# A feed-forward down projection in three parts, two of them by Strassen's seven products

## The chip, the core and the metric

The kernel runs on one core of a Trainium2 chip. A core has a matrix engine (PE) that multiplies a stationary 128x128 tile with moving columns and adds the result up in PSUM, a vector engine (DVE), an activation engine (ACT), a general engine (POOL), and a sync engine (SP) that here issues nearly all DMAs. Each has a queue of its own that runs in order; they wait for each other by semaphores. SBUF is the working memory. The metric is the time of one execution on the device in microseconds; lower is better.

## What is computed

One inference step of a one-layer decoder for 512 prompt tokens and 8 x 4 sample tokens, 544 in all, with d_model 1024 and d_ff 2816. Three token mixers run first; the change touches only the feed-forward part behind them:

```
u = _rmsnorm(x, ln_ffn) @ w_up              # (L, 1024) @ (1024, 5632)
u, ffn_conv_new = _causal_conv(u, ffn_conv, ffn_conv_w)
ua, ub = jnp.split(u + ffn_conv_b, 2, axis=-1)
x = x + ((jax.nn.silu(ua) * ub) @ w_down)   # (L, 2816) @ (2816, 1024)
return _rmsnorm(x, ln_final)
```

All data are float32.

## The kernel before

Tokens lie along the columns as two halves of 272 (256 prompt and 16 sample tokens each), features along the 128 partitions. `w_up` has 44 blocks of 128 output features with 8 k-tiles; `w_down` has 8 blocks with 22 k-tiles. The 22 feature tiles of the hidden layer are called features here: each needs two up products, one for `ua` and one for `ub`.

**A product with three matmuls.** Every float32 operand is split into a high part in the reduced type fp32r and the rest: ACT copies x to `hi`, DVE subtracts `lo = x - hi` (`split`, L252, and `wsplit`, L174, for weights). A product takes three matmuls per k-tile and half: hi·hi, hi·lo, lo·hi (`step`, L201). `gemm` (L187) does this over all k-tiles and both halves into a PSUM tile of two banks (`pm`, two such tiles); a second pool `p1` has four single banks (`bank`, L129).

**Weights.** `weights` (L159) loads up to 8 k-tiles with one DMA on SP into a `raw` tile (two buffers), and splits four k-tiles at a time into `whi` and `wlo` (four buffers each). The split of four k-tiles is one ACT and one DVE instruction of 512 columns. Loads and splits are placed ahead of their use by lowering the scheduler's priority number (`AHEAD` = 400).

**Order.** PE's instructions go in the order in which the program states them (`order`). The other queues are ordered by a list scheduler with a simulated timeline; `soon` gives what reads PSUM a priority 500 earlier. `gen` (L132) takes a scratch tile from a rotating pool `gp` of 30 in this part; `touch` (L135) writes one element of it with a POOL memset, so that POOL's queue holds the wait until that tile is free.

**The feed-forward loop** (`ffn`, L1461) has two parts of 11 features. For each feature: two up products, each with its side work (`ffn_side`, L1441: DVE scales out of PSUM into `U`, POOL copies the convolution's state in and out, ACT and two DVE instructions do the convolution), then silu on ACT, a product on DVE, and a split into `hi` and `lo`. Behind the 11 features come down products over these 11 k-tiles: all 8 blocks in the first part, blocks 0 to 5 in the second. Each result is added by DVE to the residual `xn[d]`. In the second part ACT squares the finished `xn[d]` and POOL sums the squares.

**The tail** (L1510 to L1534) does blocks 6 and 7 of the second part with the tokens in two groups of 312 and 232 columns: all matmuls of the first group, then those of the second, among which the first group's final normalisation (`final_norm`, L1543) is put at fixed points (`TK`, L1593: after k-tile 4 of block 6, and after k-tiles 1 and 2 of block 7). The second group's normalisation stands at the end by itself.

Of the kernel before, what the change touches and what calls it, by code (L numbers as in the profile page):

```python
# [9 lines left out]
F32 = mybir.dt.float32  # L10
# [12 lines left out]
NT = 4  # L23
HALF = 272
# [35 lines left out]
class Build:  # L60
# [140 lines left out]
    def step(self, o, w, r, hf, k, kt, first=True):  # L201

        (wh, wl), (rh, rl) = w, r
        self.mm(o, wh, rh[:, hf, :], start=(k == 0 and first), stop=False)
        self.mm(o, wh, rl[:, hf, :], start=False, stop=False)
        self.mm(o, wl, rh[:, hf, :], start=False, stop=(k == kt - 1))


# [1232 lines left out]
    def ffn_side(self, ps, i):  # L1441
# [17 lines left out]
        return y  # L1459

    def ffn(self):  # L1461
        self.lab = "_ff_"
        I = self.I
        KH = NPAIR // 2
        for part in range(2):
            acts = []
            for jj in range(KH):
                j = part * KH + jj
                pa = yield from self.gemm(I["wup"][j], self.h2)
                if j == 0:  # L1470
                    raw = self.gen((128, 2, HALF))
                    with self.soon():
                        self.act(raw, pa)
                    pa = raw
                    self.RB = self.rstd_rows(self.rs2, self.sqp.tile([128, 2, HALF], F32, tag="rbc", name="rbc"))
                ya = self.ffn_side(pa, j)
                pb = yield from self.gemm(I["wup"][NPAIR + j], self.h2)
                yb = self.ffn_side(pb, NPAIR + j)
                sg = self.yp.tile([128, 568], F32, tag="sg", name="sg")[:, 0:560]
                self.act(sg, ya, AF.Silu)  # L1480
                a = self.gen((128, 2, HALF))
                self.mul(a[:, :, 0:HP], self.two(sg[:, 0:512]), self.two(yb[:, 0:512]))
                vw = lambda t: t[:, 512:560].rearrange("p (a b t) -> p a b t", a=2, t=6)[:, :, :, 2:6]
                self.mul(a[:, :, HP:HALF].rearrange("p a (b t) -> p a b t", t=NT), vw(sg), vw(yb))
                hi, lo = self.gen((128, 2, HALF), F32R), self.gen((128, 2, HALF), F32R)
                self.split(a, hi, lo)
                acts.append((hi, lo))
            if part == 1:
                self.sy.dma_start(out=self.O["fc"], in_=self.fso)
                sqs = self.sqp.tile([128, 2, HALF], F32, tag="sqs", name="sqs")  # L1490
            for d in range(8 - 2 * part):
                ps = yield from self.gemm(I["wdn"][d][:, part * KH:(part + 1) * KH, :], acts)
                x = self.xn[d]
                with self.soon():
                    self.add(x, ps, x)
                if part == 0:
                    continue
                if d == 0:
# [13 lines left out]
        ds = (6, 7)  # L1512
        w = [self.weights(I["wdn"][d][:, KH:, :], KH, alt) for d in ds]
        ps = [self.pm.tile([128, 2, 512], F32, tag="mm", name="mm_fl_") for d in ds]
# [95 lines left out]
    def run(self):  # L1610
        with self.pool("cst") as self.cst, self.pool("wp") as self.wp, self.pool("hp", 8) as self.hp, \
# [15 lines left out]
            with self.pool("gp", self.NG1) as self.gp:  # L1627
# [179 lines left out]
```

## Time and profile before

| | |
|---|---|
| time, median of 3 runs | 1130.48 us (1130.06 to 1131.14) |
| profiled execution | 1130.19 us |
| its span | 1128.4 us |
| mean granted PE clock | 0.999 |
| HBM read and written | 98.93 and 11.21 MB |

The span is what the trace covers, from the first instruction to the last. A page line of busy time gives the engine, busy microseconds, the share of the span and the instructions. A row of instruction groups gives the line (often a helper's), engine, operation, output<-inputs, partitions x columns, count | busy us, mean ns of one | idle us before them and what ended the idle time. A row of windows gives the stretch, its length, and the busy us of PE, PE's weight load, DVE, ACT and POOL with their instruction counts, then the granted clock, DMA share and GB/s. A row of the chain or of the timeline gives start, length, engine, what, count. Matmuls are pipelined: one shows as about 0.29 us, but they start one behind the other at a smaller distance, so counts and stretches are used for them.

The feed-forward part runs from about 700 us on, with the stretches of up products and down products clearly apart in the slices of the page:

```profile
DVE  7886588777768657688653274476774337767533
ACT  6564344524426333353323244354443234444431
POOL 3000041100011103111321002122220012221112
PEclk9999999999999999999999999999999999999999
```

### The profile page before, as it was taken

How to read it: one execution, taken by the hardware profiler on the slowest of the kernel's cores; microseconds unless marked ns; L12 is line 12 of the kernel's file. 1: busy time of each engine (PE TensorE's matmuls, PEld its weight loads, DVE VectorE, ACT ScalarE, POOL GpSimd, SP SyncE). 2: the span in 40 equal slices, each digit the busy share in tenths (PEclk: the TensorE clock that was granted, in tenths of full speed). 3: DMA queues.
4: the chain of work that ended last, by engine and by line, in shares of the span. 5: the costliest groups of instructions: out<-in, count | busy, mean ns of one | idle time of the engine just before them, and what ended most of it. 6: DMA issues, size and time to landing. Idle time of an engine off the chain costs nothing.

```text
span 1128.4 us, 23470 instructions
## 1 busy us (share of the span) xinstructions
PE 1118.3 (99%) x9059; PEld 1101.7 (98%) x9059; DVE 732.1 (65%) x1827; ACT 466.5 (41%) x919; POOL 185.8 (16%) x664
## 2 busy tenths in 40 slices
PE   9999999999999999999999999999999999999997
PEld 8999999999999999999999999999999999999997
DVE  7886588777768657688653274476774337767533
ACT  6564344524426333353323244354443234444431
POOL 3000041100011103111321002122220012221112
PEclk9999999999999999999999999999999999999999
DMA  7233333232223334312453432323223333222332
GB/s 261 76 90 98 87 112 106 82 89 76 69 83 95 117 95 128 130 58 64 122 168 90 153 97 93 93 76 94 82 76 96 86 94 94 84 86 83 94 102 80
DMA packets 49831, 111.65 MB, mean 99 GB/s; under 512 B 11320, under 2 KB 17592, under 8 KB 49720
## 3 DMA queue, kind: packets, MB, share of 16 engines
q1 hardware_dynamic: 49000, 109.32, 31.7%
q8 instruction: 71, 1.16, 0.4%
q10 hardware_dynamic: 720, 0.84, 0.2%
q14 instruction: 40, 0.33, 0.1%
HBM read 98.93 MB, written 11.21 MB: 98 GB/s over the span
## 4 chain that ended last, share of the span: by engine, by line
PE 95%; DVE 2%; issue 1%; DMA 1%; ACT 1%; POOL 0%; SPq 0%; POOLq 0%; ACTq 0%; DVEq 0%
PE mm_fl__14143 L122 1%; PE mm_ff__11801 L122 1%; PE mm_ff__11633 L122 1%; PE mm_ff__11465 L122 1%; PE mm_ff__13687 L122 1%; PE mm_ff__14039 L122 1%; PE mm_ff__13863 L122 1%; PE mm_ff__13599 L122 1%; PE mm_ff__11297 L122 1%; PE mm_ff__13951 L122 1%; PE mm_ff__13775 L122 1%; PE mm_ff__11885 L122 1%; PE mm_ff__11717 L122 1%; PE mm_ff__11549 L122 1%; PE mm_ff__11381 L122 1%
## 5 line engine op out<-in xcount | busy, mean ns | idle before, releaser
L117 ACT ACTIVATE whi<-raw 128x512 fp32r<-128x512 f32 x320 | 199.5, 625 | 422.6 <-DMA raw<-in_wdn 11.7
L96 DVE TENSOR_TENSOR wlo<-raw,whi 128x512 fp32r<-128x512 f32 x320 | 221.1, 692 | 157.2 <-ACT whi L117 149.2
L114 DVE SCALAR_TENSOR_TENSOR y<-U,cols,y 128x560 f32<-128x560 f32 (+1 forms) x124 | 100.0, 808 | 19.0 <-ACT y L117 17.2
L117 ACT ACTIVATE y<-U,cols 128x560 f32<-128x560 f32 (+1 forms) x56 | 46.8, 838 | 23.6 <-DVE U L96 22.9
L1452 POOL COPY fso<-U 128x2 f32<-128x2 f32 x44 | 28.8, 654 | 79.6 <-DVE U L96 79.6
L1449 POOL COPY U<-fst 128x16 f32<-128x16 f32 x44 | 23.9, 546 | 81.4 <-DVE y L114 43.0
L117 ACT ACTIVATE sg<-y 128x560 f32<-128x560 f32 (+1 forms) x34 | 22.9, 675 | 21.0 <-DVE y L114 20.9
L114 DVE SCALAR_TENSOR_TENSOR col<-col,col 128x4 f32<-128x4 f32 (+3 forms) x146 | 24.7, 170 | 5.3 <-ACT junk L117 2.2
L117 ACT ACT_TABLE_LOAD x16 | 20.5, 1283 | 2.0 <-PEq L1799 0.7
L96 DVE TENSOR_TENSOR col<-col 128x4 f32<-128x4 f32 (+3 forms) x73 | 11.6, 158 | 1.3
L617 POOL COPY gso<-U 128x3 f32<-128x3 f32 x12 | 5.6, 464 | 23.0 <-ACT U L117 23.0
L111 DVE TENSOR_SCALAR col<-col 128x4 int32<-128x4 int32 (+4 forms) x32 | 6.8, 213 | 3.4 <-ACT junk L117 2.9
L96 POOL TENSOR_TENSOR tot<-tot 128x32 f32<-128x32 f32 (+5 forms) x25 | 7.8, 311 | 6.0 <-DVE gen_ph__5478 L96 3.8
L139 POOL MEMSET gen_ff__12393<- 1x1 f32 x1 | 0.1, 88 | 51.9 <-PE mm_ff__11885 L122 51.9
L1453 POOL COPY fso<-U 128x16 f32<-128x16 f32 x44 | 8.5, 193 | 0.0
L139 POOL MEMSET gen_bh__9001<- 1x1 f32 x1 | 0.1, 88 | 47.4 <-DVE gen_bh__8753 L96 47.4
L614 POOL COPY U<-gst 128x24 f32<-128x24 f32 x12 | 4.4, 373 | 20.7 <-DVE gen_g__2550 L96 8.9
L114 DVE SCALAR_TENSOR_TENSOR hlo<-xn,cols,hhi 128x544 fp32r<-128x544 f32 x8 | 6.3, 784 | 1.8 <-ACT hhi L117 1.8
L109 DVE TENSOR_SCALAR col<-col 128x4 int32<-128x4 int32 (+4 forms) x38 | 6.4, 169 | 0.7
L117 ACT ACTIVATE hhi<-xn,cols 128x544 fp32r<-128x544 f32 x8 | 6.0, 752 | 1.5 <-DVE xn L96 1.5
L122 PE MATMUL mm_fi__268<-rh 128*128 128x272 f32 x18 | 4.5, 441 | 1.3 <-DVE ones L1620 1.3
L114 DVE SCALAR_TENSOR_TENSOR xin<-xin,rp,gen_nr__470 128x544 f32<-128x544 f32 x8 | 5.7, 782 | 0.0
(5094 smaller groups left out, 4772.4 us busy)
## 6 DMA issues: line engine op xcount, KB each, us to landing
raw<-in_wp SPq DMA_DIRECT2D x47, 512.0 KB
raw<-in_wup SPq DMA_DIRECT2D x44, 512.0 KB
raw<-in_wgt SPq DMA_DIRECT2D x24, 512.0 KB
raw<-in_wdn SPq DMA_DIRECT2D x16, 512.0 KB
raw<-in_wbr SPq DMA_DIRECT2D x24, 256.0 KB
raw<-in_wout SPq DMA_DIRECT2D x8, 512.0 KB
raw<-in_wdn SPq DMA_DIRECT2D x16, 192.0 KB
xin<-in_xt SPq DMA_DIRECT2D x8, 272.0 KB
```

The source lines that it names most:

```text
L96: (eng or self.v).tensor_tensor(out=out, in0=a, in1=b, op=op)
L109: (eng or self.v).tensor_scalar(out=out, in0=a, scalar1=s1, scalar2=None, op0=op0)
L111: (eng or self.v).tensor_scalar(out=out, in0=a, scalar1=s1, scalar2=s2, op0=op0, op1=op1)
L114: self.v.scalar_tensor_tensor(out=out, in0=a, scalar=sc, in1=b, op0=op0, op1=op1)
L117: self.s.activation(out=out, in_=a, func=func, **kw)
L122: self.pe.matmul(out, lhsT=lhsT, rhs=rhs, start=start, stop=stop)
L139: self.g.memset(x[(slice(0, 1),) * len(x.shape)], 0.0)
L614: self.g.tensor_copy(out=sv[:, :, 0:3], in_=self.gst[:, tile_i, :, :])
L617: self.g.tensor_copy(out=self.gso[:, tile_i, 0, :], in_=U[:, 512:515])
L1449: self.g.tensor_copy(out=sv[:, :, 0:2], in_=self.fst[:, i, :, :])
L1452: self.g.tensor_copy(out=self.fso[:, i, 0, :], in_=U[:, 512:514])
L1453: self.g.tensor_copy(out=self.fso[:, i, 1:9, :], in_=sv[:, :, 4:6])
```

## The change

The 22 features are done in three parts of 8, 8 and 6. In the first two, the down product goes through Strassen's scheme with seven products in place of eight: two blocks of `w_down` by two k-tiles form a 2x2 matrix of 128x128 tiles, and two k-tiles by two token halves form the 2x2 matrix on the other side. For each pair of k-tiles (two features) `operands` builds seven right-hand sides: b11, b21, b22 of the activations themselves, four differences of which POOL does the subtractions, all split into `hi` and `lo`; they lie in tiles of a new pool `op` (eight tiles of 7 x 272 columns). For each pair of blocks `blocks` loads the 8 k-tiles of both blocks (one `raw` tile in `wp`, one in a new pool `wp2`, two buffers each) and forms four sums of weights, three on POOL and one on DVE. `seven` then runs the seven products, each 12 matmuls of 272 columns into one `p1` bank, with the weights' splits three products ahead. `adder` adds each product to the quarters of `xn` that need it: POOL does six additions per pair of blocks, DVE five with an operand in PSUM, ACT two copies out of PSUM.

The first feature of the next part (two up products and their side work) is moved ahead of a part's seven products. The third part's six features are split as before and its down products use `gemm` with six k-tiles; the tail has six k-tiles too. The scratch pool shrinks from 30 to 13.

```diff
+    SEVEN = ("a11", 0), ("s2", 4), ("s1", 3), ("s3", 5), ("a12", 1), ("s4", 2), ("a22", 6)
+
+    def operands(self, x0, x1, hi, lo):
+        t = self.gen((128, 2, HALF)), self.gen((128, 2, HALF))
+        b11, b12, b21, b22 = x0[:, 0, :], x0[:, 1, :], x1[:, 0, :], x1[:, 1, :]
+        self.sub(t[0][:, 0, :], b12, b11, self.g)
+        self.sub(t[0][:, 1, :], b22, t[0][:, 0, :], self.g)
+        self.sub(t[1][:, 0, :], b22, b12, self.g)
+        self.sub(t[1][:, 1, :], b21, t[0][:, 1, :], self.g)
+        self.split(b11, hi[:, 0, :], lo[:, 0, :])
+        self.split(x1, hi[:, 1:3, :], lo[:, 1:3, :])
+        self.split(t[0], hi[:, 3:5, :], lo[:, 3:5, :])
+        self.split(t[1], hi[:, 5:7, :], lo[:, 5:7, :])
+
+    def blocks(self, src1, src2, q):
+        p = self.tc.cur_priority
+        self.at(p - self.AHEAD - 400)
+        raw = [pool.tile([128, 8, 128], F32, tag="raw", name="raw", bufs=2) for pool in (self.wp, self.wp2)]
+        for r, src in zip(raw, (src1, src2)):
+            self.sy.dma_start(out=r[:, :2 * q, :], in_=src)
+        b = {"a%d%d" % (i + 1, j + 1): raw[i][:, j:2 * q:2, :] for i in range(2) for j in range(2)}
+        self.at(p - self.AHEAD - 20)
+        for n, x, y, eng in (("s1", "a21", "a22", self.g), ("s2", "s1", "a11", self.v), ("s3", "a11", "a21", self.g),
+                             ("s4", "a12", "s2", self.g)):
+            b[n] = self.gen((128, 4, 128))[:, :q, :]
+            self.tt(b[n], b[x], b[y], ALU.add if n == "s1" else ALU.subtract, eng)
+        self.at(p)
+
+        def split():
+            for n, _ in self.SEVEN:
+                p = self.tc.cur_priority
+                self.at(p - self.AHEAD)
+                w = self.wsplit(b[n])
+                self.at(p)
+                yield w
+        return split()
+
+    def seven(self, src1, src2, rhs, take):
+        q = len(rhs)
...
+        sp = self.blocks(src1, src2, q)
+        ws = [next(sp) for _ in range(3)]
+        for n, i in self.SEVEN:
+            w = ws.pop(0)
+            b = self.bank()[:, :HALF]
+            for k in range(q):
+                wh, wl = w[k]
+                rh, rl = (r[:, i, :] for r in rhs[k])
+                self.mm(b, wh, rh, start=k == 0, stop=False)
+                self.mm(b, wh, rl, start=False, stop=False)
+                self.mm(b, wl, rh, start=False, stop=k == q - 1)
...
+            with self.soon():
+                take(n, b)
+            w = next(sp, None)
+            if w:
+                ws.append(w)
+
+    def adder(self, x):
+        t = self.gen((128, 2, HALF)), self.gen((128, 2, HALF))
+        s1, u2, u3, s5 = t[0][:, 0, :], t[0][:, 1, :], t[1][:, 0, :], t[1][:, 1, :]
+        def take(n, b):
+            if n == "a11":
+                self.act(s1, b)
+                self.add(x[0], x[0], s1, self.g)
+            elif n == "s2":
+                self.add(u2, b, s1)
+                self.add(x[1], x[1], u2, self.g)
+            elif n == "s1":
+                self.act(s5, b)
+                self.add(x[1], x[1], s5, self.g)
+                self.add(x[3], x[3], s5, self.g)
+            elif n == "s3":
+                self.add(u3, b, u2)
+                self.add(x[2], x[2], u3, self.g)
+                self.add(x[3], x[3], u3, self.g)
+            else:
+                o = x[{"a12": 0, "s4": 1, "a22": 2}[n]]
+                self.add(o, b, o)
+        return take
...
+    PARTS = 8, 16, 22
+
     def ffn(self):
...
-        KH = NPAIR // 2
-        for part in range(2):
+        op = lambda: self.op.tile([128, 7, HALF], F32R, tag="op", name="op")
+        a, j0 = {}, 0
+        for end in self.PARTS:
             acts = []
...
+            last = end == NPAIR
+            for j in range(j0, end):
+                if j not in a:
+                    a[j] = yield from self.ffn_up(j)
+                if last:
...
+                    self.split(a[j], hi, lo)
+                    acts.append((hi, lo))
+                elif j % 2:
+                    acts.append((op(), op()))
+                    self.operands(a[j - 1], a[j], *acts[-1])
+            KH = end - j0
+            if not last:
+                a[end] = yield from self.ffn_up(end)
+                for d in range(0, 8, 2):
+                    x = [self.xn[e][:, hf, :] for e in (d, d + 1) for hf in range(2)]
+                    yield from self.seven(*(I["wdn"][e][:, j0:end, :] for e in (d, d + 1)), acts, self.adder(x))
+                j0 = end
+                continue
...
-            for d in range(8 - 2 * part):
-                ps = yield from self.gemm(I["wdn"][d][:, part * KH:(part + 1) * KH, :], acts)
+            for d in range(6):
+                ps = yield from self.gemm(I["wdn"][d][:, j0:end, :], acts)
...
-        w = [self.weights(I["wdn"][d][:, KH:, :], KH, alt) for d in ds]
+        w = [self.weights(I["wdn"][d][:, j0:, :], KH, alt) for d in ds]
...
-            with self.pool("gp2", 30) as self.gp, self.pool("sqp") as self.sqp, self.pool("fc") as fc:
+            with self.pool("gp2", 13) as self.gp, self.pool("op", 8) as self.op, self.pool("wp2", 2) as self.wp2, \
+                    self.pool("sqp") as self.sqp, self.pool("fc") as fc:
```

`ffn_up`, which is new as a function, holds the lines L1469 to L1484 of before unchanged.

More of the change, by code (lines that the diff above doesn't have):

```diff
@@ new lines, in seven @@
+    def seven(self, src1, src2, rhs, take):
+        q = len(rhs)
+        lab = self.lab
+        sp = self.blocks(src1, src2, q)
[9 more added lines that the diff above has]
+                self.mm(b, wl, rh, start=False, stop=k == q - 1)
+                if k % 2:
+                    yield
+            with self.soon():
[3 more added lines that the diff above has]
+                ws.append(w)
+        self.lab = lab
@@ L1459, in ffn_side, with ffn_up @@
         return y
+    def ffn_up(self, j):
+        I = self.I
+        pa = yield from self.gemm(I["wup"][j], self.h2)
+        if j == 0:
+            raw = self.gen((128, 2, HALF))
+            with self.soon():
+                self.act(raw, pa)
+            pa = raw
+            self.RB = self.rstd_rows(self.rs2, self.sqp.tile([128, 2, HALF], F32, tag="rbc", name="rbc"))
+        ya = self.ffn_side(pa, j)
+        pb = yield from self.gemm(I["wup"][NPAIR + j], self.h2)
+        yb = self.ffn_side(pb, NPAIR + j)
+        sg = self.yp.tile([128, 568], F32, tag="sg", name="sg")[:, 0:560]
+        self.act(sg, ya, AF.Silu)
+        a = self.gen((128, 2, HALF))
+        self.mul(a[:, :, 0:HP], self.two(sg[:, 0:512]), self.two(yb[:, 0:512]))
+        vw = lambda t: t[:, 512:560].rearrange("p (a b t) -> p a b t", a=2, t=6)[:, :, :, 2:6]
+        self.mul(a[:, :, HP:HALF].rearrange("p a (b t) -> p a b t", t=NT), vw(sg), vw(yb))
+        return a
+    PARTS = 8, 16, 22
     def ffn(self):
@@ L1463, in ffn @@
         I = self.I
-        KH = NPAIR // 2
-        for part in range(2):
+        op = lambda: self.op.tile([128, 7, HALF], F32R, tag="op", name="op")
+        a, j0 = {}, 0
+        for end in self.PARTS:
             acts = []
[L1467 to L1490, printed above, removed]
-            for d in range(8 - 2 * part):
-                ps = yield from self.gemm(I["wdn"][d][:, part * KH:(part + 1) * KH, :], acts)
@@ new lines, in ffn @@
+            last = end == NPAIR
[3 more added lines that the diff above has]
+                if last:
+                    t, i = divmod(j - j0, 3)
+                    if i == 0:
+                        hl = op(), op()
+                    hi, lo = (x[:, 2 * i:2 * i + 2, :] for x in hl)
+                    self.split(a[j], hi, lo)
[3 more added lines that the diff above has]
+                    self.operands(a[j - 1], a[j], *acts[-1])
@@ new lines, in ffn @@
+            KH = end - j0
[6 more added lines that the diff above has]
+                continue
+            self.sy.dma_start(out=self.O["fc"], in_=self.fso)
+            sqs = self.sqp.tile([128, 2, HALF], F32, tag="sqs", name="sqs")
@@ L1495, in ffn @@
                     self.add(x, ps, x)
-                if part == 0:
-                    continue
                 if d == 0:
```

## The prediction

> **What bounds the kernel now.** I read the page's busy shares first, then the matrix engine's (PE's) own waits, then two stretches of windows (a down stage, an up stage), then the chain that ended last.
>
> ```profile
> PE 1118.3 (99%) x9059; PEld 1101.7 (98%) x9059; DVE 732.1 (65%) x1827; ACT 466.5 (41%) x919; POOL 185.8 (16%) x664
> PE mm_fi__268 L122 <- DVE ones L1620: 1.3, 1, 1.3
> 860.00:900.00 40.00, 40.00 (x322) 40.00 (x321) 13.06 (x20) 8.94 (x15) 0.00 (x0) 1.00 0.30 87
> 980.00:1020.00 40.00, 40.00 (x319) 40.00 (x318) 28.63 (x51) 18.26 (x27) 8.61 (x22) 1.00 0.29 92
> 908.65 8.24 PE mm_ff__11885 L122 x66
> 1044.00 6.05 PE mm_ff__13511 L122 x48
> 1050.06 7.51 PE mm_ff__13599 L122 x60
> 1066.57 8.24 PE mm_ff__13775 L122 x66
> 1099.57 4.73 PE mm_fl__14143 L122 x33
> 1104.30 4.68 PE mm_fl__14144 L122 x33
> 1108.98 1.67 PE mm_fl__14143 L122 x15
> 1111.89 2.12 PE mm_fl__14143 L122 x18
> ```
>
> PE is busy 99% of the span and its longest wait, 1.3 us, lies in the first stage. In both stretches PE is full at clock 1.00, DVE works 33% of the down stage (13.06 of 40) and 72% of the up stage, POOL nothing and 22%. So PE instructions are the price: a 272-column matmul costs 8.24/66 = 0.125 us in the down stage, a 312-column one 4.73/33 = 0.143, a 232-column one 1.67/15 = 0.111. The first two down products of the second part take 1066.57 - 1050.06 = 16.51 us for 132 matmuls, 0.125 each: no stall lies at that transition now.
>
> **The matmuls removed.** Before: part 1 has 8 blocks x 11 k-tiles x 2 halves x 3 = 528, part 2 six blocks, 396, the tail (blocks 6 and 7) 66 of 312 and 66 of 232 columns. After: two parts of 4 pairs x 7 products x 4 k-pairs x 3 = 336 each, 6 x 36 = 216 in the third, a tail of 36 and 36. That is 924 - 888 = 36 fewer of 272 columns (4.5 us), 30 fewer of 312 (4.3) and 30 of 232 (3.3): **-12.1 us**, if PE stays full. A pair of blocks takes 84 x 0.125 = 10.5 us, a product 1.5.
>
> **What is added beside PE.** These rows price it; the timeline rows give start, length and engine.
>
> ```profile
> L96 DVE TENSOR_TENSOR wlo<-raw,whi 128x512 fp32r<-128x512 f32 x304 | 212.3, 699 | 135.1 <-ACT whi L117 127.2 <-ACT rbc L117 3.8 <-PE mm_ff__9649 L122 0.2
> L117 ACT ACTIVATE whi<-raw 128x512 fp32r<-128x512 f32 x304 | 191.2, 631 | 398.0 <-DMA raw<-in_wdn 11.2 <-issue 7.6 <-PE mm_bg__7796 L122 6.6
> L96 POOL TENSOR_TENSOR xn<-xn,gen_fn__14240 128x312 f32<-128x312 f32 x3 | 2.5, 860 | 0.7 <-ACT gen_fn__14240 L117 0.7
> L96 POOL TENSOR_TENSOR xn<-xn,gen_fn__14346 128x232 f32<-128x232 f32 x3 | 1.9, 674 | 4.1 <-ACT gen_fn__14346 L117 4.1
> L96 POOL TENSOR_TENSOR sqs<-sqs,gen_ff__13755 128x544 f32<-128x544 f32 x1 | 1.4, 1362 | 11.4 <-ACT gen_ff__13755 L117 11.4
> L96 DVE TENSOR_TENSOR xn<-mm_fl__14143,xn 128x312 f32<-128x312 f32 x1 | 0.5, 483 | 4.0 <-PE mm_fl__14143 L122 4.0
> L117 ACT ACTIVATE gen_fn__14240<-bank_fn__14291 128x312 f32<-128x312 f32 x1 | 0.4, 432 | 1.0 <-DVE xn L114 1.0
> 583.93 0.68 DVE L96 TENSOR_TENSOR wlo<-raw,whi 128x512 fp32r<-128x512 f32 x1
> 584.10 1.74 POOL L96 TENSOR_TENSOR acc<-acc,gen_bg__8012 128x544 f32<-128x544 f32 x1 [3.76 <-DVE gen_bg__8012 L96]
> 565.55 1.60 DVE L96 TENSOR_TENSOR wlo<-raw,whi 128x512 fp32r<-128x512 f32 x1 [1.13 <-ACT whi L117]
> 565.58 1.03 POOL L96 TENSOR_TENSOR gen_h__8002<-kuv,cf 128x512 fp32r<-128x512 f32 x1
> 561.03 0.72 DVE L96 TENSOR_TENSOR gen_bg__7732<-mm_bg__7741,gen_bg__7732 128x544 f32<-128x544 f32 x1 [3.88 <-PE mm_bg__7741 L122]
> 560.75 1.04 POOL L96 TENSOR_TENSOR gen_h__7835<-kuv,cf 128x512 fp32r<-128x512 f32 x1
> ```
>
> Per pair of blocks (10.5 us of PE). ACT: 7 whi x 0.63 + 2 evictions of about 0.4 = 5.2, hidden. DVE: 7 wlo x 0.70, s2 another 0.70, five evictions of 272 columns from PSUM at about 0.44 (below the 0.483 of 312) = 7.8: 74%, as the up stage bears now without a PE wait. POOL: a 272-column addition lies between 674 and 860 ns, 0.77; 512 columns just under 1362, about 1.3; three sums and six additions make 8.5 us, 81%.
>
> Each fits alone. Together they may not: a wlo and a POOL addition shut each other out. The POOL addition of 584.10 needs 1.36 alone but ended at 585.84, 1.23 after the wlo ended (584.61). The wlo of 565.55 took 1.60 because POOL was reading until 566.61, and ended 0.54 later. DVE instructions with an operand in PSUM don't suffer: that of 561.03 ran its 0.72 beside POOL's of 560.75. So the held times add: POOL 1.23 per 544 columns, thus 0.62 for 272 and 1.16 for 512, 6 x 0.62 + 3 x 1.16 = 7.2; DVE 8 x 0.55 = 4.4. Sum **11.6 us per pair against PE's 10.5**; with the whole durations it would be 8.5 + 5.6 = 14.1.
>
> [...]
>
> Against the excess stands lead: the three weight splits ahead are 4.5 us of PE work, and the first pair's sums (3 x 1.16 + 0.55 = 4.0) can run under the up product moved ahead of it. A part then needs 4 x 11.6 - 4.0 = 42.4 against 42.0, nearly balanced; queues in order never use such a port without holes, and the moved product's side work (28.63 of 40 on DVE) competes at the start. I take **+3.0** for both parts, nearest to the held times; bounds 0 and, by whole durations, 2 x (4 x 14.1 - 4.6 - 42.0) = 20.
>
> **Operands.** Per pair of features: four POOL subtractions (3.1 us in 24.2 of PE), ACT and DVE 1904 columns instead of 1088, about 1.1 us more each; DVE in the up stage goes from 72% to 76%. Cost 0: the up product moved ahead (12.1 us of PE) covers the last pair's operands, whose chain now takes 6.4 us from the matmuls' end to the split's (1050.16 to 1056.55, rows below) and gets 2.3 of POOL and 1.9 of splits longer. Without that cover it would be up to 10 per part.
>
> **DMA.** The same bytes, now two of 512 KB per pair, 100 GB/s against 87. The moved product's two loads stand ahead of the pair's on SP's queue, as any up product's do now.
>
> ```profile
> L167 SPq DMA_DIRECT2D raw<-in_wdn x28: 327/328/336, 855.2 to 1094.0; - x28
> 1097.26 1.57 ACT L117 ACTIVATE whi<-raw 128x512 fp32r<-128x512 f32 x3 [3.67 <-DMA raw<-in_wdn]
> 1050.16 0.79 DVE L96 TENSOR_TENSOR U<-mm_ff__13511,rbc 128x512 f32<-128x512 f32 x2 [1.40 <-PE mm_ff__13511 L122]
> 1053.70 0.69 DVE L96 TENSOR_TENSOR wlo<-raw,whi 128x512 fp32r<-128x512 f32 x1
> 1055.82 0.73 DVE L96 TENSOR_TENSOR gen_ff__13577<-gen_ff__13571,gen_ff__13575 128x544 fp32r<-128x544 f32 x1 [0.72 <-ACT gen_ff__13575 L117]
> 1112.82 0.36 DVE L114 SCALAR_TENSOR_TENSOR col<-col,col 128x3 f32<-128x3 f32 x2
> 1116.37 1.89 DVE L114 SCALAR_TENSOR_TENSOR xn<-xn,cols,bank_fn__14291 128x312 f32<-128x312 f32 x4 [0.50 <-ACT gen_fn__14240 L117]
> 1118.40 0.40 DVE L96 TENSOR_TENSOR xn<-mm_fl__14144,xn 128x232 f32<-128x232 f32 x1
> ```
>
> The load issued last (1094.0) landed by 1097.26, 3.3 us; a buffer here is asked for some 10 us ahead. Cost 0.
>
> **The last transition.** The third part has six k-tiles. Its first down product needs the newest feature's second operand at its 32nd matmul, 31 x 0.125 = 3.9 us after its start; with eleven k-tiles that was 61 x 0.125 = 7.6. That operand is written at 1055.82 + 0.73 = 1056.55, 6.5 us after the start at 1050.06. The work was hidden; the cover goes: **+2.6** (1.9 if the wlo of 1053.70 moves behind, 3.5 if POOL gets in the way).
>
> **The tail.** The second token group now has 36 matmuls, not 66, over the first group's normalisation. Its scale is ready at 1113.18, 4.2 after the group began, while PE comes to it at 1.7 + 1.3 + 0.3 + 0.7 = 4.0 (fifteen matmuls, the sums until 1111.89, three, six): 0.3 with the handover. The first group's DVE scalings (1.89) now stand about where the last addition becomes ready, and POOL's multiplications beside the small column work: about 1.2. **+1.5**, bounds 0.5 and 2.5.
>
> **Sum.** -12.1 + 3.0 + 2.6 + 1.5 = -5.0. The profiled execution took 1130.19 (span 1128.4, 1.8 around it), 0.3 below the median 1130.48. So 1125.2 on its scale, **1125.5** as a median.
>
> **Rivals.**
>
> *Nothing stalls in the Strassen stages*: the lead and the holes left by up products hold all of it. For it: DVE at 72% never makes PE wait now. Against it: 11.6 is over 10.5. It gives 1122.5; 0.20.
>
> *The port decides.* If the turns cost whole durations (14.1 per pair), the splits fall behind PE from the second pair on, when the 4.5 us of lead are spent at 3.6 per pair. For it: POOL goes from 0.00 of 40 to 81% in this stage, and POOL instructions back to back kept a wlo out for 1.05 us. Against it: the held times are shorter. Price -12.1 + 20 + 2.6 + 1.5 = +12: 1142, and 1132.5 at half of the 20. From a stall of 10.3 us in both parts, 1.3 per pair, it is slower than before; 0.20.
>
> *The smaller scratch pool.* Scratch tiles go from 30 to 13, which two pairs fill (six each) beside the feature held over; each is first touched by a POOL memset, which waits in POOL's queue:
>
> ```profile
> L139 POOL MEMSET gen_ff__12393<- 1x1 f32 x1 | 0.1, 88 | 51.9 <-PE mm_ff__11885 L122 51.9
> ```
>
> 51.9 us waited there, with nothing behind it; now the sums and additions stand behind. If that adds 0.6 per pair to the port's loss, 8 x 0.6 = 5 us, the gain is gone: 1130; 0.15.
>
> **How the numbers follow.** Forecast (1123.5 to 1128) 0.45, no stall 0.20, scratch pool 0.15, port 0.20. The measurement tells about 0.2%, 2.3 us, from no change. Faster 0.65, same 0.15, slower 0.20. The range is 1121 (no stall, transition 1.9, tail 0.5) to 1134, the port rival at a good half of its price; about 0.2 lies outside.
>
> **What would show it.** Right: 960 matmuls in the down stages and tail, 1.5 us per product, a pair in 10.5 to 11; POOL near 80% there; wlo and POOL additions longer than 0.70 and 0.77; a PE gap of 2.6 in the third part's first down product. Wrong: PE waits on wlo or whi summing over 10 us, evictions behind POOL, memsets waiting with additions queued, or gaps of PE at the Strassen stages' first product.

## The result: 1137.5 us, slower than before

| | before | after |
|---|---|---|
| time, median (lowest to highest) | 1130.76 us (1130.06 to 1131.14) | 1137.49 us (1137.17 to 1138.65) |
| profiled execution; its span | 1130.19; 1128.4 | 1137.17; 1135.4 |

After over before is 1.0062, with an interval of 1.0045 to 1.0080. The forecast was 1125.5, its range ended at 1134: the sign was wrong, and the time lies outside the range.

The page of the changed kernel, busy times first, then the slices of DVE and POOL, then the group of the weights' splits:

```profile
PE 1114.4 (98%) x8963; PEld 1094.5 (96%) x8963; DVE 802.9 (71%) x1907; ACT 490.5 (43%) x975; POOL 302.8 (27%) x788
DVE  7886588767768656798653374578897778976753
POOL 3000041000011112111410001134587344781213
L96 DVE TENSOR_TENSOR wlo<-raw,whi 128x512 fp32r<-128x512 f32 (+1 forms) x312 | 226.3, 726 | 119.7 <-ACT whi L117 112.0
```

The 96 matmuls are gone (9059 before, 8963 now), yet PE's busy time fell by 3.9 us only, and the span grew by 7.0. POOL's two tall places in the slices are the two Strassen stages. The row of splits mixes two widths (726 ns); those of 512 columns alone, 304 before and after, went from 699 to 735 ns over the whole kernel.

A Strassen stage holds 28 products of twelve matmuls, 42.0 us at 0.125 each. By the starts of their first matmuls in the timeline, the first stage ran from 825.75 to 876.14 and the second from 973.00 to 1023.60: 50.4 and 50.6 us. **So 8.4 and 8.6 us are lost there, 17.0 in all, where 3.0 was forecast.** PE's own waits in the first stage (in total, times, longest), then windows of it (sum of the stretch, then PE, PEld, DVE, ACT and POOL busy, clock, DMA share, GB/s):

```profile
PE bank_ff__11403 L122 <- DVE xn L96: 2.2, 1, 2.2
PE bank_ff__11403 L122 <- DVE wlo L96: 1.0, 1, 1.0
PE bank_ff__11079 L122 <- DVE wlo L96: 0.8, 1, 0.8
PE bank_ff__11133 L122 <- DVE wlo L96: 0.4, 1, 0.4
PE bank_ff__11147 L122 <- DVE wlo L96: 0.4, 1, 0.4
```

```profile
826.00:868.00 42.00, 37.01 (x272) 35.60 (x271) 36.42 (x49) 17.41 (x32) 35.61 (x52) 0.96 0.25 76
854.00:856.70 2.70, 0.55 (x5) 0.33 (x3) 2.17 (x3) 0.92 (x2) 2.14 (x5) 1.00 0.00 0
856.70:860.20 3.50, 2.48 (x13) 2.28 (x14) 3.50 (x4) 0.08 (x1) 3.50 (x5) 0.82 0.00 0
860.20:862.60 2.40, 2.40 (x13) 2.40 (x13) 2.40 (x4) 0.55 (x1) 2.35 (x4) 0.56 0.66 218
862.60:866.00 3.40, 3.40 (x30) 3.40 (x29) 2.93 (x6) 1.54 (x3) 3.00 (x6) 1.00 0.55 154
```

Splits that came late make up 2.6 us of these waits; the largest wait is for an eviction. POOL is busy 35.61 of 42 us (85%), DVE 36.42 (87%), and behind the long gap PE runs 2.40 us in which it gets 13 matmuls done, at a clock of 0.56, where it has room for 19. The second stage has the same gap (2.3 us, before the bank numbered 13219).

What led to it is in the timeline of POOL and DVE (start, length, engine, what, and in brackets the idle time before it and its releaser):

```profile
846.38 2.41 POOL L96 TENSOR_TENSOR xn<-xn,gen_ff__11161 128x272 f32<-128x272 f32 x2
848.87 3.46 POOL L96 TENSOR_TENSOR xn<-xn,gen_ff__11163 128x272 f32<-128x272 f32 x3
852.33 0.76 POOL L96 TENSOR_TENSOR xn<-xn,gen_ff__11163 128x272 f32<-128x272 f32 x1
853.21 1.28 POOL L96 TENSOR_TENSOR gen_ff__11473<-raw 128x512 f32<-128x512 f32 x1
```

```profile
850.80 0.91 DVE L96 TENSOR_TENSOR wlo<-gen_ff__11321,whi 128x512 fp32r<-128x512 f32 x1
854.52 1.74 DVE L96 TENSOR_TENSOR gen_ff__11476<-gen_ff__11473,raw 128x512 f32<-128x512 f32 x1 [2.82 <-POOL gen_ff__11473 L96]
856.19 0.43 DVE L96 TENSOR_TENSOR xn<-bank_ff__11299,xn 128x272 f32<-128x272 f32 x1
856.54 1.62 DVE L96 TENSOR_TENSOR wlo<-gen_ff__11327,whi 128x512 fp32r<-128x512 f32 x1
```

Read it backwards. PE waits for a PSUM bank. The bank is freed by the eviction at 856.19, 0.43 us of DVE work that stands behind the second sum (`s2`, at 854.52). `s2` needs the first sum (`s1`, POOL, 853.21), and `s1` stands behind six additions that POOL began at 846.38 and ended at 853.1: 6.63 us for six, 1.1 each. DVE idled 2.8 us meanwhile with splits and an eviction queued behind `s2`. **In the third pair, a wait that crosses from DVE to POOL and back came on top of the late splits that I had counted.**

### The profile page after: what moved, and what is told of

Same layout as the page of the kernel before. It is cut to its first block, busy times and chain, and to the rows that moved or that the text cites. A ratio compares the mean times of both kernels' runs of the same rounds, so it can differ in the third digit from the quotient of the medians.

```text
span 1135.4 us, 23576 instructions
## 1 busy us (share of the span) xinstructions
PE 1114.4 (98%) x8963; PEld 1094.5 (96%) x8963; DVE 802.9 (71%) x1907; ACT 490.5 (43%) x975; POOL 302.8 (27%) x788
## 4 chain that ended last, share of the span: by engine, by line
PE 89%; DVE 5%; POOL 3%; issue 2%; ACT 1%; DMA 0%; SPq 0%; POOLq 0%; DVEq 0%; ACTq 0%
POOL xn L96 2%; DVE wlo L96 1%; PE mm_pg__2310 L122 1%; PE mm_pm__427 L122 1%; PE mm_ph__5632 L122 1%; PE mm_ph__5499 L122 1%; PE mm_pg__2497 L122 1%; PE mm_bm__3098 L122 1%; PE mm_pm__733 L122 1%; PE mm_pg__2094 L122 1%; PE mm_pg__2191 L122 1%; PE mm_ff__9655 L122 1%; PE mm_ff__9737 L122 1%; PE mm_ph__6119 L122 1%; PE mm_pg__2682 L122 1%
## 5 line engine op out<-in xcount | busy, mean ns | idle before, releaser
L117 ACT ACTIVATE whi<-raw 128x512 fp32r<-128x512 f32 (+1 forms) x312 | 194.3, 625 | 375.2 <-issue 8.6
L96 DVE TENSOR_TENSOR wlo<-raw,whi 128x512 fp32r<-128x512 f32 (+1 forms) x312 | 226.3, 726 | 119.7 <-ACT whi L117 112.0
L1543 POOL COPY U<-fst 128x16 f32<-128x16 f32 x44 | 21.1, 482 | 65.2 <-DVE y L114 40.1
L117 ACT ACT_TABLE_LOAD x16 | 20.5, 1283 | 2.0 <-PEq L1916 0.7
L1547 POOL COPY fso<-U 128x16 f32<-128x16 f32 x44 | 13.8, 313 | 0.0
L122 PE MATMUL mm_fl__14493<-op,whi 128*128 128x312 f32 (+2 forms) x36 | 6.8, 296 | 0.0
L122 PE MATMUL mm_fl__14494<-op,whi 128*128 128x312 f32 (+1 forms) x24 | 6.0, 342 | 0.0
```

The lines of the kernel that those rows point to most:

```text
L96: (eng or self.v).tensor_tensor(out=out, in0=a, in1=b, op=op)
L117: self.s.activation(out=out, in_=a, func=func, **kw)
L122: self.pe.matmul(out, lhsT=lhsT, rhs=rhs, start=start, stop=stop)
L1543: self.g.tensor_copy(out=sv[:, :, 0:2], in_=self.fst[:, i, :, :])
L1547: self.g.tensor_copy(out=self.fso[:, i, 1:9, :], in_=sv[:, :, 4:6])
```

## The experiments

Two theories of the 17.0 us. *Port*, the prediction's word: POOL's additions and DVE's splits come out longer where they overlap (its rows have a POOL addition of 1.74 us against 1.36 and a split of 1.60 against 0.70), and that decides. *Queue*: POOL's additions, however long, stand ahead of the sums of the next pair, and DVE waits for these. A third question is the tail. "Stalls" below is a stage's length less 42.0, for the first and the second Strassen stage, from the run's profiled execution. Executions also differ ahead of the change: the feed-forward part starts at 714.4 us before, at 717.3 in e2's profile and at 714.1 in e9's, so a median holds some us that a stall doesn't.

| run | median (lowest to highest), us | ratio to before, interval | stalls |
|---|---|---|---|
| the changed kernel | 1137.49 (1137.17–1138.65) | 1.0062, 1.0045–1.0080 | 8.4, 8.6 |
| e1_s1_dve | 1130.32 (1129.05–1131.82) | 0.9998, 0.9988–1.0008 | 4.5, 4.6 |
| e7_sums_later | 1137.86 (1136.37–1138.46) | 1.0065, 1.0048–1.0082 | 8.2, 8.1 |
| e2_no_adds | 1128.21 (1126.15–1130.23) | 0.9978, 0.9967–0.9989 | 3.1, 3.2 |
| e3_adds_aside | 1137.46 (1136.21–1139.18) | 1.0065, 1.0049–1.0080 | 9.3, 8.2 |
| e4_memsets_aside | 1127.34 (1125.57–1128.69) | 0.9971, 0.9962–0.9981 | 5.0, 3.0 |
| e9_hold_short | 1127.07 (1125.88–1128.09) | 0.9970, 0.9958–0.9982 | 3.1, 2.9 |
| e10_hold_long | 1134.25 (1131.27–1136.43) | 1.0035, 1.0023–1.0047 | 4.8, 5.6 |
| e11_hold_long_s1 | 1128.38 (1127.75–1131.51) | 0.9986, 0.9977–0.9996 | 3.4, 3.4 |
| e5_plain_parts | 1133.97 (1132.14–1135.04) | 1.0033, 1.0019–1.0048 | – |
| v1_late_adds | 1134.06 (1133.17–1134.69) | 1.0038, 1.0023–1.0053 | 6.3, 7.2 |
| v2_late_adds_s1 | 1133.19 (1131.17–1135.78) | 1.0027, 1.0015–1.0039 | 6.4, 6.5 |
| v9_three_adds | 1129.58 (1127.77–1131.40) | 0.9988, 0.9980–0.9997 | 4.3, 4.2 |
| v10_three_adds_s2 | 1132.90 (1130.13–1133.29) | 1.0010, 1.0001–1.0018 | 5.7, 4.8 |
| t1_tail_later | 1135.86 (1135.20–1137.11) | 1.0043, 1.0028–1.0059 | 8.4, 8.6 |
| v12_adds_tail | 1127.36 (1126.50–1129.72) | 0.9975, 0.9966–0.9984 | 4.4, 3.6 |

### The sum that crosses (e1, e7)

e1 gives the first sum to DVE:

```diff
-        for n, x, y, eng in (("s1", "a21", "a22", self.g), ("s2", "s1", "a11", self.v), ("s3", "a11", "a21", self.g),
+        for n, x, y, eng in (("s1", "a21", "a22", self.v), ("s2", "s1", "a11", self.v), ("s3", "a11", "a21", self.g),
```

> One edit: the weight sum s1 is formed by DVE instead of POOL; the rest is the changed kernel. Queue theory (the loss comes mainly from DVE's s2, which stands in DVE's queue in front of an eviction and of weight splits and waits for POOL's s1, itself behind six POOL additions): the 2.8 us DVE wait in the third pair goes, and with it PE's gap and the low clock behind it, 5.2 us per part: about 1127. Port theory (POOL and DVE simply need more time on the shared port than PE needs): s1 costs the port 0.6 us less per pair, 5 us at most over eight pairs: 1133 to 1136. If DVE becomes the bound (8.5 of 10.5 us per pair): 1137 or more.

e7 asks whether the sums are only issued too early or too late:

```diff
-        self.at(p - self.AHEAD - 20)
+        self.at(p - 60)
```

> One edit to the changed kernel: the four weight sums of a pair are placed 60 priority steps ahead of the pair instead of 420; s1 stays on POOL. Queue theory: DVE's s2 then stands behind the last pair's evictions and splits and no longer holds them up while it waits: the 2.8 us wait and the low clock go, 1125 to 1131, unless the sums become late for their own splits. Port theory: the port's work is the same, 1134 to 1138.

e1 took 7.2 us off, and the wait on the eviction is gone. In the 42 us from 826 on POOL's additions took 1.14 us and the splits 0.99 us on average, as in the changed kernel, so it wasn't shorter instructions that gained this. POOL also has one sum less per pair, for which the expectation allowed 5 us at most; by that estimate at least 2 of the 7.2 are the crossing wait's. PE's two longest waits in e1's first stage are for splits:

```profile
PE bank_ff__11251 L122 <- DVE wlo L96: 0.8, 1, 0.8
PE bank_ff__11231 L122 <- DVE wlo L96: 0.8, 1, 0.8
```

But 4.5 us per stage remain, more than expected. e7 changed nothing, and its trace shows why: on POOL `s1` still stands behind the same six additions, on DVE `s2` still ahead of the same eviction, and DVE still idles 2.8 us there. So 360 steps of priority didn't move the sums in the queues, and e7 tests neither theory.

### What of an addition costs (e2, e3, e4, e9, e10, e11)

e2 leaves POOL's additions out; e3 keeps them but writes into an unused tile, so that no DVE addition waits for their result:

```diff
-                self.add(x[0], x[0], s1, self.g)
+                self.add(dump, x[0], s1, self.g)
```

> The changed kernel without POOL's six additions to xn per pair of blocks (left out; DVE's additions stay). POOL keeps the three weight sums, 3.9 of 10.5 us per pair. If POOL's additions, by queue or by port, make the loss in the two Strassen stages (17 us in the trace): nearly all of it goes, 1121 to 1124. If the loss has another source (loads, DVE's own time, scratch tiles): 1130 or more.

> POOL does the six additions with the same reads, but writes the results to an unused tile: xn gets only DVE's additions, and no DVE instruction waits for a POOL addition. Port and queue theories alike: POOL's queue is as long as before and stands in front of s1 as before, 1134 to 1138. If the direct wait of DVE's additions for POOL's (same quarter of xn) makes the loss: 1121 to 1127.

e3 equals the changed kernel, so the order of additions on `xn` isn't a cause. Without the additions the kernel takes 1128.2; they cost 9.3 us. But 1128.2 lies above the 1121 to 1124 of the expectation: stalls of 3.1 and 3.2 us, 6.3 of the 17.0, remain without any addition. In e2's first stage PE waits 0.7 us for a split of the first pair, which stands on DVE behind the last operands' split, the second sum and the moved product's side work, and 1.0 and 0.3 us in the third pair. Do the additions cost their 9.3 us by their reads, or by POOL's time? e4 was meant to tell:

```diff
-                self.add(x[0], x[0], s1, self.g)
+                [self.g.memset(self.identr.bitcast(F32)[:, 0:m], 0.0) for m in (576, 160)]
```

> As the run with additions aside, but each addition is replaced by two POOL memsets of 576 and 160 columns (about 0.75 us together, as long as an addition of 272 alone), which read nothing from SBUF; the additions are left out. Port theory: POOL's work per pair is as long on paper, but neither it nor DVE's weight splits are held up, so additions of 1.2 us become 0.75 and wlo stays at 0.69: 1122 to 1128. If POOL's own time and the queue order make the loss without the port: as the run with additions aside, within 3 us.

It took 1127.34, which looks like a clean answer for the port. It is none. The tile's own view (duration ns least/median/most, first and last start) shows where these memsets ran (two of its six rows):

```profile
L287 POOL MEMSET identr<- x16: 231/406/590, 560.8 to 617.2; 128x576 f32 x8, 128x160 f32 x8
L298 POOL MEMSET identr<- x16: 228/406/594, 572.4 to 621.8; 128x576 f32 x8, 128x160 f32 x8
```

They waited for nothing, so they were done by 622 us, 200 us before the stage. e4's stages run without additions as e2's do. (Its first stage stalled 5.0 us where e2's stalled 3.1; why isn't shown.) So e9 and e10 tie POOL's work to its place with a copy of one column of the addition's operand, then two or three memsets; e11 is e10 with `s1` on DVE:

```diff
+        def hold(t):
+            self.g.tensor_copy(out=z[:, 0:1], in_=t[:, 0:1])
+            for m in (272, 272, 272):
+                self.g.memset(z[:, 0:m], 0.0)
...
-                self.add(x[0], x[0], s1, self.g)
+                hold(s1)
```

> Edit: each of POOL's six additions of a pair becomes a copy of one column of its operand, which pins the place, and two memsets of 272 columns, about 0.7 to 0.8 us, an addition's time when nothing shares the port; the output lacks those additions. Port theory: a memset reads nothing, splits stay near 0.70, stalls of 3 to 4 per stage as without additions, about 1128. Queue theory (POOL's time alone delays the next pair's sums): POOL's work is what the forecast gave it, 8.5 us of 10.5 a pair, and the stalls are 4 to 6 per stage, 1129 to 1132.

> Edit: as before with three memsets of 272 columns, 1.1 to 1.2 us in the place of each addition, which is what the additions took in the changed kernel. Port theory: without the additions' reads the splits stay near 0.70 and the stages stall by 3 to 5 each, 1128 to 1131. Queue theory: POOL is as busy as in the changed kernel, the first sum of the third pair comes as late and DVE's second sum and the eviction behind it with it: stalls of 8 per stage, 1136 to 1138.

> Edit: the three memsets in each addition's place, and the first sum of each pair on DVE. Port theory: the 4.5 us per stage that were left with the first sum on DVE were splits lengthened by additions; without their reads 1 to 3 per stage are left, 1124 to 1128. Queue theory: nothing waits for POOL's first sum in either, and the splits were late for DVE's own load and late loads: 4 to 5 per stage, about 1130.

The groups of POOL's and DVE's work in the same 42 us (busy us, mean ns, idle before): of e9, of e10, and of the changed kernel with two of its six groups of additions.

```profile
L287 POOL MEMSET cf<- 128x272 f32 x40 | 13.1, 328 | 2.1
L96 DVE TENSOR_TENSOR wlo<-raw,whi 128x512 fp32r<-128x512 f32 x12 | 9.3, 774 | 1.6 <-ACT whi L117 1.5
```

```profile
L287 POOL MEMSET cf<- 128x272 f32 x48 | 15.7, 327 | 2.2
L96 DVE TENSOR_TENSOR wlo<-raw,whi 128x512 fp32r<-128x512 f32 x11 | 7.5, 682 | 1.5 <-ACT whi L117 1.5
```

```profile
L96 POOL TENSOR_TENSOR xn<-xn,gen_ff__11011 128x272 f32<-128x272 f32 x4 | 4.8, 1230 | 0.0
L96 POOL TENSOR_TENSOR xn<-xn,gen_ff__11163 128x272 f32<-128x272 f32 x4 | 4.2, 1074 | 0.0
L96 DVE TENSOR_TENSOR wlo<-raw,whi 128x512 fp32r<-128x512 f32 x10 | 9.2, 921 | 0.8 <-ACT whi L117 0.8
```

The rows of splits hold those of loaded weights only. Over all splits in the window, those of the sums too, the mean is 0.99 us in the changed kernel, 0.83 in e9 and 0.81 in e10.

A copy took 0.18 to 0.73 us, 0.4 on average, so a hold was about 1.05 us in e9 and 1.4 in e10. The changed kernel's eighteen additions in this window took 20.5 us, 1.14 each. Holding POOL for 1.05 us in the additions' place costs nothing (1127.07; 1128.2 without additions). Holding it for 1.4, longer than the additions do, gives 1134.25, still 3.2 us below the changed kernel, and its profiled execution with the stalls of 4.8 and 5.6 is among its fastest (1131.4).

The crossing wait itself is there in both. The second sum and PE's wait for the eviction behind it, first of e9, then of e10:

```profile
852.20 0.69 DVE L96 TENSOR_TENSOR gen_ff__11512<-gen_ff__11509,raw 128x512 f32<-128x512 f32 x1 [3.25 <-POOL gen_ff__11509 L96]
PE bank_ff__11435 L122 <- DVE xn L96: 0.3, 1, 0.3
852.93 1.76 DVE L96 TENSOR_TENSOR gen_ff__11530<-gen_ff__11527,raw 128x512 f32<-128x512 f32 x1 [3.11 <-POOL gen_ff__11527 L96]
PE bank_ff__11451 L122 <- DVE xn L96: 1.2, 1, 1.2
```

DVE idles 3.25 and 3.11 us for `s1`, longer than the 2.82 of the changed kernel, but PE waits 0.3 and 1.2 us for the eviction in place of 2.2: in e9 and e10 the sum came earlier against PE's products. Part of that is which of two overlapping sums starts first. In the changed kernel `s2` came 0.06 us behind POOL's third sum (854.52 and 854.46) and took 1.74 us; in e10 0.08 behind it (852.85) and took 1.76; in e9 0.04 ahead of it (852.24) and took 0.69.

So POOL's time without the additions' reads can cost some 7 us when it is longer than the additions were; at a little less than theirs it was free. Of the 10.4 us from e9 to the changed kernel, 3.2 are left for the additions' reads (the two inputs of 272 columns that a memset lacks) by the comparison with e10. That is an estimate and not a bound, because the holds didn't all stay where the additions were: ahead of the `s1` of the timeline above stand 5.9 us of holds in e9, 5.8 in e10, and 6.6 of additions in the changed kernel. The reads also fit the step from 0.76 us, the addition of 852.33 with DVE idle, to 1.14 on average, while the memsets took 0.33 each in e9 and e10 alike. **Additions and splits came out longer together (1.14 us against 0.76, 0.99 against 0.81 to 0.84), and in the changed kernel POOL's queue hands that on to `s1`, `s2` and what stands behind them.** With no crossing sum, e11 against e1, the additions' reads cost 1.9 us. How the 7 us between e9 and e10 would divide at exactly 1.14 us, and which wait makes them, isn't settled.

### The new parts and the tail (e5, t1)

e5 keeps the parts of 8, 8 and 6 features but computes them with plain products, and moves no up product ahead:

```diff
-                if last:
+                if True:
...
             if not last:
...
+                for d in range(8):
+                    ps = yield from self.gemm(I["wdn"][d][:, j0:end, :], acts)
+                    with self.soon():
+                        self.add(self.xn[d], ps, self.xn[d])
+                j0 = end
+                continue
```

> The three parts of 8, 8 and 6 features kept, with plain products in all three and no up product moved ahead: 1056 matmuls as before the change. It prices the shorter last part and tail alone. Strassen stages are the cause of the loss: 1130.8 plus 2 to 3 for the tail, 1131 to 1134. The split into parts is the cause: 1137 or more.

It is 3.5 us slower than before, with no Strassen product in it. PE's only waits over 0.3 us from 700 us on are in the tail:

```profile
PE bank_fn__14285 L122 <- ACT gen_fn__14273 L117: 1.5, 1, 1.5
PE bank_fn__14240 L122 <- DVE col L114: 0.5, 1, 0.5
```

The tail, from the first 232-column matmul to the end of the span, is 18.78 us in e5 and 19.58 before; with 30 matmuls fewer at 0.111 us it would be 16.3. So the shorter tail costs some 2.5 of the 3.5 us by itself. t1 moves two steps of the first group's normalisation behind later k-tiles in the changed kernel:

```diff
-    TK = ((0, 4), (1, 1), (1, 2))
+    TK = ((0, 4), (1, 3), (1, 4))
```

> Edit: the changed kernel, but two PE steps of the first token group's normalisation are put behind the second group's fourth and fifth k-tile of the second block, not behind its second and third. If the tail's loss is PE waiting for the scale in the middle of the second group (0.5 us at the column, and the clock behind it), the tail from the second group's start to the end of the span is 17.5 to 18.0 us in place of 18.5 and the time falls by 0.5 to 1. If the loss is that the first group's scalings and outputs no longer have enough matmuls over them, later steps make them later: 18.5 to 19.2, and the time is the same or up to 0.7 longer. The rest of the kernel is as in the changed one, 1137.

The tail is 18.67 us in the changed kernel and 16.89 in t1: 1.8 gained, more than expected. First PE's timeline and windows of the changed kernel, then both of t1 (windows as above):

```profile
1121.40 1.24 PE L122 MATMUL bank_fn__14596<-cf,col 128*128 128x128 f32 x6 [0.49 <-DVE col L114]
```

```profile
1121.40:1123.00 1.60, 1.60 (x9) 1.60 (x10) 0.32 (x1) 0.00 (x0) 0.49 (x1) 0.61 0.00 0
1123.00:1125.20 2.20, 2.20 (x13) 2.20 (x12) 1.70 (x5) 0.43 (x1) 1.44 (x2) 0.51 0.22 81
```

```profile
1121.50 0.86 PE L122 MATMUL bank_fn__14602<-cf,col 128*128 128x128 f32 x6
```

```profile
1121.40:1123.00 1.60, 1.60 (x17) 1.59 (x15) 0.56 (x2) 0.04 (x1) 0.57 (x1) 1.00 0.00 0
```

PE idled 0.49 us for the scale's column, and the clock then stood at 0.61 and 0.51 until 1125.2, so that the last twelve matmuls of the group came 0.21 us apart in place of 0.11. In t1 the column is ready when PE comes to it, the clock stays at 1.00, and the group ends 2.2 us earlier.

But the low clock isn't where most of the 1.8 us come from. e9 has the changed kernel's tail and the same wait of 0.49 us, its clock stayed at 1.00 from 1110 to 1118 (its last matmuls of the group 0.11 us apart), and its tail took 18.31 us all the same. DVE's timeline of e9 and of t1 shows what does it:

```profile
1112.71 1.89 DVE L114 SCALAR_TENSOR_TENSOR xn<-xn,cols,bank_fn__14692 128x312 f32<-128x312 f32 x4 [0.50 <-ACT gen_fn__14656 L117]
1114.52 0.39 DVE L96 TENSOR_TENSOR xn<-mm_fl__14590,xn 128x232 f32<-128x232 f32 x1
```

```profile
1123.12 0.40 DVE L96 TENSOR_TENSOR xn<-mm_fl__14494,xn 128x232 f32<-128x232 f32 x1 [0.19 <-PE mm_fl__14494 L122]
1123.44 1.88 DVE L114 SCALAR_TENSOR_TENSOR xn<-xn,cols,bank_fn__14602 128x312 f32<-128x312 f32 x4
```

In e9 the first group's four scalings stand ahead of the second group's last addition. The last matmul for it started at 1112.76, and the addition began at 1114.52, 8.43 us after the group's start. In t1 the addition goes first, 6.31 us after the group's start. e1, e5, v9 and e10 have the 0.49 us wait, clock 1.00 over the group, and 8.42 or 8.43; the changed kernel has 8.79, so its low clock is worth about 0.4 us of the tail.

### Other divisions of the work (v1, v2, v9, v10, v12)

v1 has DVE form all intermediate sums from the PSUM banks, and POOL only two additions of 544 columns per pair at the end; v2 is v1 with the first sum on DVE:

```diff
+            elif n == "s3":
+                self.add(v, b, w)
+                self.add(y2, b, y2)
...
+            elif n == "s4":
+                self.add(w, b, w)
+                self.add(x[0], x[0], t[0], self.g)
+            else:
+                self.add(y2, b, y2)
+                self.add(x[1], x[1], t[1], self.g)
```

> The adder rewritten: DVE adds each product out of PSUM to intermediate sums only (seven instructions per pair in place of five, one ACT copy in place of two), and POOL adds two finished 544-column tiles to xn in place of six additions of 272. No DVE instruction waits for a POOL addition, and POOL reads 4 us less long per pair by whole durations. s1 stays on POOL. Queue theory: POOL's queue before s1 is short, the DVE wait in the third pair goes: 1121 to 1127. Port theory: 2 x 1.23 + 3 x 1.16 + 4.4 = 10.3 us per pair against 10.5: 1121 to 1126. DVE as the bound (8.7 us of its own per pair): above 1130.

> Both edits: the rewritten adder and s1 on DVE. DVE 9.4 us of its own per pair against 10.5, port 2 x 1.23 + 2 x 1.16 + 9 x 0.55 = 9.7. Queue theory: no worse than the rewritten adder alone, 1119 to 1124. If DVE becomes the bound: slower than the rewritten adder alone, 1126 to 1132.

v1 lies 7 us or more above the ranges of both theories; only its third case, DVE as the bound (above 1130), fits its time, and DVE was busy 38.60 of the 42 us from 826 on. v2 lies 9 us above its first range and 1 above its second, and isn't slower than v1. v2's timeline shows what took the additions' place:

```profile
853.04 0.69 DVE L96 TENSOR_TENSOR gen_ff__11464<-raw 128x512 f32<-128x512 f32 x1 [1.42 <-DMA raw<-in_wdn]
855.35 1.81 DVE L96 TENSOR_TENSOR wlo<-gen_ff__11315,whi 128x512 fp32r<-128x512 f32 x1
854.84 1.77 POOL L96 TENSOR_TENSOR xn<-xn,gen_ff__11158 128x544 f32<-128x544 f32 x1
```

This is the fourth pair's first sum. It waited for its weights, whose buffer comes free only after the last split of the second pair (there are two buffers). Then a split of the third pair and a wide addition of the second met, at 1.8 us each, and PE waited 2.5 us for this split. That fewer and wider additions are worse for coming at the end of a pair fits this; no run shows it by itself.

v9 takes the first sum and three of the six additions to DVE, straight from the PSUM bank; v10 the same three additions, with all four sums on POOL:

```diff
-                self.add(x[0], x[0], s1, self.g)
+                self.add(x[0], b, x[0])
...
-                self.act(s5, b)
-                self.add(x[1], x[1], s5, self.g)
-                self.add(x[3], x[3], s5, self.g)
+                self.add(x[1], b, x[1])
+                self.add(x[3], b, x[3])
```

> Edit: the first sum of each pair on DVE, and three of POOL's six additions go to DVE, straight from the PSUM bank (the product a11 into its output, the product s1 into its two), so that POOL keeps two sums and three additions a pair. Port theory: by the held times a pair now has 3 x 0.62 + 2 x 1.16 on POOL and 9 x 0.55 on DVE, 9.1 us against PE's 10.5 (11.0 with all six additions and the first sum on DVE), so the stages stall by 3 to 3.5 us each in place of 4.5, and the time is about 1128. Rival, DVE is the bound: its own work is now 9 x 0.70 + 8 x 0.44 = 9.8 of 10.5 us, 94%, so splits come late and the stages stall by 5 or more each, 1131 or above.

> Edit: the same three additions go to DVE, but all four sums are on POOL, so that no sum crosses from one queue to the other and back. Port theory: POOL 3 x 0.62 + 4 x 1.16 and DVE 7 x 0.55, 10.3 us a pair, closer to PE's 10.5: stalls of 4.5 to 6 per stage, 1130 to 1132. Queue theory (what cost was one engine's sum waiting behind the other engine's queue): both engines have slack, DVE 80% and POOL 72%, and nothing crosses: 3 per stage or less, about 1127.

v9 is 0.12% faster than before, with 4.3 and 4.2 us of stalls: between what the port theory and its rival gave, at DVE 40.63 of 42 us in the window. v10 has 5.7 and 4.8, as the port's held times gave, but it isn't free of crossing either. No sum crosses, yet a DVE addition to a quarter of `xn` waits for POOL's addition to the same quarter, which stands behind POOL's sums (the releaser shown is the memset right behind that addition, of 861.35):

```profile
862.13 0.79 DVE L96 TENSOR_TENSOR xn<-bank_ff__11381,xn 128x272 f32<-128x272 f32 x2 [1.38 <-POOL gen_ff__11911 L139]
```

PE's three longest waits in v10's first stage, 1.5, 1.1 and 0.8 us, are for evictions to `xn`. So v10 doesn't part the theories. Beside e1, half the additions gone from POOL (v9) is worth 0.7 us, which is within what the runs can tell.

v12 is v9 with t1's edit:

> Edit: the kernel with three additions on DVE and the first sum on DVE, and the later steps of the first group's normalisation in the tail. If the stages' losses and the tail's are separate terms, the tail's 1.8 us come off whole: the tail takes 16.7 to 17.2 us in place of 18.8, and the time is 1127.3 to 1128.3 (1129.6 without the edit), about 0.3% below the kernel before. Rival: the tail's gain hung on the lower clock or on the state in which the slower stages left the queues; then less than 0.8 comes off, 1128.8 or above.

1127.36: the tail's gain comes off whole, its tail is 16.87 us (18.78 in v9, whose clock was at 1.00 over the second group, so the gain doesn't hang on the low clock). **It beats the kernel before by 0.25% (0.16 to 0.34) and the changed one by 0.9%.** Its account closes: -12.1 for the matmuls, +8.0 in the stages, +0.6 in the tail and +0.2 at the last transition make -3.3; its span is 3.6 shorter than before.

## Why the prediction was wrong, point by point

**The matmuls (-12.1): right.** 8963 are left, and where nothing waits a product takes 1.5 us; the fourth pair of the first stage, which has no next pair's sums beside it, ran its seven in 10.5.

**The Strassen stages (+3.0): this step failed.** I wrote that "the held times add" and took "+3.0 for both parts, nearest to the held times"; 17.0 was measured. Two things were mis-sized. First, an addition beside splits doesn't cost its held 0.62, nor its own 0.77: it stood in POOL's queue for 1.14, waits included, and that is what POOL's queue has to carry. Second, I looked for the loss in late splits alone. From start to start, a product that waited shows its whole loss, which is more than its row of waiting. Of the first stage's 8.4 us, the late splits of the first two pairs cost 3.1 (the products around these waits took 2.56, 4.30 for two, 2.04 and 1.66 in place of 1.5 each). The other 5.2 lie in three products of the third pair (3.89, 3.34 and 2.51 over 4.5): 2.4 for the eviction behind `s2`, 1.2 for a split that stood behind the same `s2`, and 1.6 for the low clock behind that gap. The upper bound, 20, did hold the 17. The range did not, because it took the port rival at a good half of its price. Without any addition (e2) 6.3 of the 17.0 were left, so even these were above the 3.0.

**The rival "the port decides" came nearest,** at 17 of its 20 us, but the size is partly luck: it came by another road than "the splits fall behind PE from the second pair on". I gave it 0.20.

**Operands (0): right.** No PE wait lies in the up stages or at a Strassen stage's first product. But an operands' split on DVE at 823.99, 1.80 us long, stood ahead of the split that the first pair's third product waited for.

**DMA (0): nearly right.** In the changed kernel the one wait for a load in the first stage is 0.7 us on POOL. Where the other waits were taken away it came up: 1.19 us in e1, 1.42 in v2.

**The last transition (+2.6): wrong.** It cost 0.2. The chain of the changed kernel:

```profile
1084.29 3.77 PE mm_ff__14171 L122 x30
1088.05 3.75 PE mm_ff__14223 L122 x30
1093.49 4.78 PE mm_ff__14275 L122 x36
```

I had PE stand at the first block's sixth k-tile. It takes five k-tiles of the first block (30 matmuls), then five of the second, and the sixth ones after these: 9.2 us for 72 matmuls, 9.0 without a wait. The order was in the trace of before as well, and I had read the groups' totals only.

**The tail (+1.5): the place right, the size too small.** Of 3.3 us of matmuls saved in the second group, 0.9 was gained, so 2.4 was lost. I had counted 0.3 for the scale's column and about 1.2 for the scalings. The wait for the column was 0.49, the last addition waited about 1.5 behind the four scalings (e9, at full clock), and the low clock added about 0.4. t1, with the addition ahead of the scalings, took 1.8 back.

**The smaller scratch pool: not seen.** The longest wait of a POOL memset in the first stage is 1.0 us, and PE's longest wait leads to additions, not to a memset. A larger pool wasn't tried, so a share of the small pool isn't excluded.

The sum as measured: -12.1 + 17.0 + 0.2 + 2.4 = +7.5, against a span 7.0 longer. The feed-forward part starts 0.7 us earlier than before (713.71 and 714.42), ahead of anything changed, which leaves 0.2.

## What to carry to other kernels

When instructions of two engines come out longer side by side, charge each what it occupies its queue for, waits included, and then ask what stands behind it: here POOL could be held for 1.05 us per addition free of charge, while additions that took 1.14, beside splits of 0.99 in place of 0.83, cost 10.4 us, and 7.2 came back when one sum no longer crossed to POOL and back (e1). Look for such crossings in what the additions write, too: v10 took out one and kept another. And before reading a control run as an answer, find its instructions in the trace: one that waits for nothing runs somewhere else (e4), and a changed priority may leave the queues as they were (e7).

## What the runs showed of the hardware

**Behind three gaps of PE the clock stood near 0.5 for 3 us or more.** Behind the 2.2 us wait of the first stage the clock was still 1.00 until 858.8, and then 0.51 from 859.2 to 862.4; behind the 2.3 us of the second it was 0.50 from 1006.0 to 1009.0; after the 0.49 us in the tail, with matmuls of 232 columns ahead of it, it was 0.52 from 1121.6 to 1125.0. It doesn't always happen: the same 0.49 us left the clock at 1.00 over the group in e1, e5, v9, e9 and e10, and 0.8 us at 829 left it there in the changed kernel. What decides isn't shown. In the first stage the low clock cost 1.6 us, behind listed waits of 3.2.

**Beside POOL's additions DVE's splits were longer, beside its memsets not.** All splits of the window took 0.83 and 0.81 us on average beside memsets (e9, e10), 0.84 with nothing in the additions' place (e2), and 0.99 beside additions; the group of the loaded weights' splits on the page has 716, 704, 702 and 726 ns in the same order. An addition took 1.14 us on average, against 0.76 for the one of 852.33 with DVE idle, and 1.8 us passed on either side where a split met an addition of 544 columns (v2).
